# Hybrid decoder trunk on one core: queries and one more convolution projection by seven block products, query and key norms rearranged

## The chip, the core and the metric

The kernel runs on one core of a Trainium2 chip. A core has a matrix engine (TensorE, in the profile PE, with its weight loads as PEld), three engines for element-wise work (VectorE or DVE, ScalarE or ACT, GpSimd or POOL), a queue engine (SyncE or SP) and 16 DMA engines. Each engine works through its own list of instructions and waits for others by semaphores. The metric is the device time of one execution in microseconds; the shown time is the median of three runs.

## What is computed

Two layers. In each, a normalised input (512 tokens, 2048 channels) goes through one wide projection; three groups of heads (a short gated convolution, stick-breaking attention, gated linear attention) work on its parts, each result is gated, and an output projection adds it to the residual.

```python
h = rmsnorm(x, norm_g);  proj = h @ w_in                     # 2048 -> 7696 columns
y_conv = b * (conv3(c * h_) + bias) * silu(cv_g)             # 512 channels, width 3, causal
q = rmsnorm(sb_q, sb_qn_g); k = rmsnorm(sb_k, sb_kn_g)       # 8 heads of 128
z = (q * 128**-0.5) @ k.T                                    # in blocks of 128 queries, strictly causal
log_keep = where(mask, log_sigmoid(-z), 0)
later = reverse_cumsum(log_keep) - log_keep
w = where(mask, exp(log_sigmoid(z) + later), 0)
y_sb = (w @ v) * silu(sb_g)
y_gla = rmsnorm(gla(gl_q, gl_k, gl_v, decay)) * silu(gl_g)   # chunks of 64, with a state
out = x + concat(y_conv, y_sb, y_gla) @ w_out
```

All inputs and outputs are float32.

## The kernel before

**Projections.** Every operand of a projection is split into two float16 parts (high and low), and a product is three matmuls: high x high, high x low, low x high. A projection takes 256 output columns of a weight matrix ("v 0", "g 0", "conv h 1" and so on). Plain, it is 192 matmuls of 256 columns with tokens as rows (`project_toks`, through `tok_mm`, L683 to L685), or 96 of 512 columns with channels as rows (`project_cols`, L673 to L675). The projections named in `QUICK` and `QUICK_IN` go by seven block products in place of eight (`project_quick`, with `prod` at L764 for channels and L767 for tokens): 168 matmuls of 256 columns, or 336 of 128. Seven products need sums of the quarters of the weights (`wsums`), sums of the quarters of the input, made once per layer (`xsums`), and sums of the results (L778 to L792: three copies on ACT and five sums on DVE). In the input projection these are g, k of all four attention blocks, and "conv h 1".

**Weights.** A tile of weights (2 MB) is fetched from POOL's queue two projections ahead, into one of two buffers (`fetch`, L355). ACT sums its squares (L366), POOL reduces over partitions (L380), DVE makes the scale (L383 to L398). Then it is split: plain as two halves of 128x2048 (ACT L435, DVE L442); for seven products as seven parts of 128x1024 (ACT L485, DVE L486) with one accumulating DMA inside SBUF (L503) and three sums on DVE (L506, L508, L511). The parts lie in three pairs of buffers plus one (`w7h`, `w7l`), which the next projection's parts take as the matmuls free them.

**An attention block** (`for j in range(4)`) projects v, g, q and k of two heads. The squares of q and k are summed per head and token on ACT (L1318). `rsqrt_bits` makes the inverse roots on DVE from the bits of the number and three Newton steps (L211 to L218), once for q and once for k, eight columns each. q is multiplied by its roots (L1327), k by its roots and by `kg`, the product of the two norm weights (L1332, eight instructions). Both are split into float16 parts in one buffer, `qp`, (L1336, L1337) and transposed by DMA on SP (L1341). `attend` queues four steps that later projections start by `go()`: scores of each head and values of each head. Scores: query tiles are taken in two groups (`CHUNKS`): tiles 3 and 2 together (896 columns) and tiles 0 and 1 (384). Matmuls (L1226), a mask (L1230), two sigmoids per group with one scale per layer (L1234, L1236), a running product from the right (L1239), products and a split (L1241 to L1245), eight DMA transposes per block on SP (L1247). Values: matmuls (L1263) and a multiplication with the gate per group (L1270).

**The later convolution** (`conv_in(1)`, `conv_out(1)`) follows the last block: "conv h 1", "conv c 1", "conv g 1", "conv b 1". After the first of these `mixload` fetches the mixed results of the branches back from DRAM by six copies on SP (L887) into the buffers that hold `xsums`' sums until then. Before the output projection `weight_ratio` scales them (L1150, L1151).

**Order.** Apart from a part at the start that is written out by hand, a planner puts each engine's instructions into order at compile time, by its own estimate of times and by priorities (weights come first); on the chip the order is fixed.

Of the kernel before, what the change touches and what calls it, by code (L numbers as in the profile page):

```python
# [30 lines left out]
QUICK_IN = ("g 0", "k 0", "g 1", "k 1", "g 2", "k 2", "g 3", "k 3", "conv h 1")  # L31
# [5 lines left out]
TWICE = ("wm", "wgm", "wq", "ws", "wp", "vu", "bm", "bsmix", "gsmix", "lr", "xr0", "xrm", "xrt", "xtot", "xrstd", "xrs")  # L37


CHUNKS = ((((3, 0), (2, 512)), (3, 2)), (((0, 0), (1, 128)), (0, 1)))  # L40
# [3 lines left out]
def hybrid_trunk(ctx, tc, x, norm_g, w_in, conv_w, conv_b, sb_qn_g, sb_kn_g,  # L44
# [163 lines left out]
    def rsqrt_bits(dst, src, scale, n, tag):  # L208

        m = sm(n, tag + "rm")  # L210
        V.tensor_scalar(m, src, scale, EPS, ALU.mult, ALU.add)  # L211
        r = sm(n, tag + "r0")
        V.tensor_scalar(r.bitcast(I32), m.bitcast(I32), -0.5, float(0x5F375A86), ALU.mult, ALU.add)
        t = sm(n, tag + "rt")
        for i in range(3):
            V.tensor_tensor(t, r, r, ALU.mult)
            V.scalar_tensor_tensor(t, t, -0.5, m, ALU.mult, ALU.mult)
            V.scalar_tensor_tensor(dst if i == 2 else r, t, 1.5, r, ALU.add, ALU.mult)  # L218
# [68 lines left out]
    def layer_consts():  # L287
# [3 lines left out]
        for l in range(depth):  # L291
# [11 lines left out]
            V.tensor_scalar(gq[:, 0:1], gq[:, 0:1], gq[:, 1:2], 2.0 ** -10, ALU.mult, ALU.mult)  # L303
# [353 lines left out]
    for l in range(depth):  # L657
# [497 lines left out]
        def conv_in(j, then=lambda: None):  # L1155
# [5 lines left out]
            if j:  # L1161
                mixload()
# [3 lines left out]
            for c in range(2):  # L1166
                V.scalar_tensor_tensor(uc[:, c, :], ps[c], u, hb[:, c, :], ALU.mult, ALU.mult)
            y = wk([P, 2, seq], "kT")
# [45 lines left out]
        def attend(j, qT, kT, vh, vl, vu, g, s_):  # L1214
# [3 lines left out]
            def scores(hh):  # L1218

                th[hh] = wk([P, 2, 10, P], "th", 2, F16)  # L1220
                for n, (qtiles, _) in enumerate(CHUNKS):
# [12 lines left out]
                    S.activation(a, z[:, :zw], AF.Sigmoid, scale=nzun[:, l:l + 1])  # L1234
                    w = wk([P, zw], "zw")
                    S.activation(w, z[:, :zw], AF.Sigmoid, scale=zun[:, l:l + 1])  # L1236
# [12 lines left out]
            def values(hh):  # L1249
# [17 lines left out]
                for n, (_, cols) in enumerate(CHUNKS):  # L1267
                    q0 = min(cols)
                    a = op[:, 2 * n:2 * n + 2, :]
                    V.scalar_tensor_tensor(y[:, q0:q0 + 2, :], a[:, ::-1, :] if cols[0] > cols[1] else a, vu[:, 1:2],  # L1270
                                           g[:, hh, q0 * P:(q0 + 2) * P].rearrange("p (t c) -> p t c", c=P),
                                           ALU.mult, ALU.mult)
# [4 lines left out]
        for j in range(4):  # L1277
# [20 lines left out]
            for gain in (None, kg[:, l, :]):  # L1298
                raw = []

                def dst():
                    raw.append(wk([P, NT, GW], *(("raw", 1) if gain is None else ("kT",))))
# [7 lines left out]
                sq = sm(8, "qs")  # L1310
                for b in range(2):
# [4 lines left out]
                    for i in range(4):  # L1316
                        cs = slice(i * P, (i + 1) * P)
                        S.activation(e[:, cs], rb.rearrange("p a c -> p (a c)")[:, cs], AF.Square,  # L1318
                                     accum_out=sq[:, 4 * b + i:4 * b + i + 1])
                u2 = sm(1, "qu2")  # L1320
                V.tensor_scalar(u2, u, u, 1.0 / P, ALU.mult, ALU.mult)
                rs = sm(8, "qr")
                rsqrt_bits(rs, sq, u2, 8, "q")
                V.tensor_scalar(rs, rs, u, None, ALU.mult)
                if gain is None:
                    r8 = raw.rearrange("p a (h c) -> p (a h) c", c=P)
                    V.tensor_tensor(r8, r8, rs.rearrange("p (a o) -> p a o", o=1).to_broadcast([P, 8, P]), ALU.mult)  # L1327
                else:
                    for t in range(NT):
                        for hh in range(2):  # L1330
                            rp = raw[:, t, hh * P:(hh + 1) * P]
                            V.scalar_tensor_tensor(rp, rp, rs[:, 2 * t + hh:2 * t + hh + 1], gain, ALU.mult, ALU.mult)  # L1332

                top = 2.0 ** 10 if gain is None else 1.0
# [4 lines left out]
                nT_ = wk([P, 2, NT, 2, P], "kT" if qkT else "qT", dt=F16)  # L1339
# [4 lines left out]
            attend(j, *qkT, vh, vl, vu, g, s_)  # L1344
# [86 lines left out]
```

## Time and profile before

| | us |
|---|---|
| median of three runs (lowest, highest) | 1716.04 (1715.94, 1717.55) |
| profiled execution | 1717.69 |
| its span, from the first to the last instruction | 1715.9 |
| PE busy in it | 1669.9 |
| DVE busy | 1331.3 |
| ACT busy | 1129.1 |
| POOL busy | 239.2 |

Mean granted TensorE clock in the span: 0.992.

How to read the rows below. A row of a group is: line, engine, operation, out<-in by the program's names, shapes and count | busy us in total, mean ns of one | idle time of the engine just before them and what ended most of it. A row of the chain or of a timeline is: start in us from the span's start, duration, engine, line. A row of stages gives the stretch, its length, the busy us of each engine with its number of instructions, the granted clock, the share of the DMA engines and GB/s. Matmuls overlap in PE's pipeline: one of 256 columns is listed with 273 ns, but the next one starts 109 ns after it, so pace is read from starts.

### The profile page before, as it was taken

To read this page: it belongs to the slowest core of one execution; us is meant where nothing else is said; L and a number is where in the kernel's file an instruction comes from. 1 tells how busy PE (TensorE), PEld (TensorE's weight loads), DVE (VectorE), ACT (ScalarE), POOL (GpSimd) and SP (SyncE) were. 2 spreads that over 40 slices of the span, in tenths; PEclk is the share of its full clock that TensorE was granted. 3 is DMA by queue.
4 is the path that set the end of the run, shared out by engine and by line. 5 is a ranking of instruction groups with operands and counts; after the bars stand their busy time and mean duration, and the time that the engine had idled before them with its cause. 6 is when DMAs were issued, how large, how long until landed. Compare 5 with 4: busy or idle time off the path is not lost.

```text
span 1715.9 us, 36876 instructions
## 1 busy us (share of the span) xinstructions
PE 1669.9 (97%) x15642; PEld 1298.4 (76%) x15642; DVE 1331.3 (78%) x2327; ACT 1129.1 (66%) x1619; POOL 239.2 (14%) x286
## 2 busy tenths in 40 slices
PE   7999999999999989999989999999999999899999
PEld 5644548989898964799976455689898889548998
DVE  8975889877878767785688677997786888677883
ACT  7667677767666656666665676776765767565662
POOL 1211111111111111001122101121111111101110
PEclk9999999999999999999999999999999999999999
DMA  7233323566766686245543332446666667753441
GB/s 251 83 114 98 99 64 99 145 116 152 136 149 139 147 233 164 77 150 181 186 103 108 116 102 75 118 123 125 148 136 105 146 132 150 201 153 108 162 151 50
DMA packets 181478, 227.26 MB, mean 132 GB/s; under 512 B 94194, under 2 KB 141628, under 8 KB 180800
## 3 DMA queue, kind: packets, MB, share of 16 engines
q0 software_dynamic: 60352, 168.83, 34.4%
q1 hardware_dynamic: 111952, 46.61, 14.4%
q10 hardware_dynamic: 9008, 9.45, 1.7%
q8 instruction: 122, 2.00, 0.5%
q14 instruction: 44, 0.36, 0.1%
HBM read 179.65 MB, written 14.68 MB: 113 GB/s over the span
## 4 chain that ended last, share of the span: by engine, by line
PE 73%; DVE 12%; DMA 7%; ACT 4%; issue 3%; POOL 0%; DVEq 0%; ACTq 0%
PE psp L767 13%; PE psp L674 8%; PE psp L675 8%; PE psp L673 8%; PE psp L685 7%; PE psp L684 7%; PE psp L683 7%; PE psp L814 6%; PE psp L764 3%; DMA st<-in_w_in_dram 2%; DVE wl L486 2%; DMA th<-za 2%; DMA kT<-qp 2%; ACT junk L366 1%; DVE wl L442 1%
## 5 line engine op out<-in xcount | busy, mean ns | idle before, releaser
L366 ACT ACTIVATE junk<-st 128x2048 uint8<-128x2048 f32 x150 | 285.1, 1901 | 44.1 <-DMA st<-in_w_in_dram 42.8
L442 DVE SCALAR_TENSOR_TENSOR wl<-st,ws,wh 128x2048 f16<-128x2048 f32 x102 | 239.2, 2347 | 80.7 <-ACT wh L435 80.7
L435 ACT ACTIVATE wh<-st,ws 128x2048 f16<-128x2048 f32 x100 | 199.3, 1998 | 105.4 <-PE psp L674 47.1
L684 PE MATMUL psp<-wl,m 128*128 128x256 f16 x960 | 261.7, 273 | 0.0
L683 PE MATMUL psp<-wh,m 128*128 128x256 f16 x960 | 261.7, 273 | 0.0
L685 PE MATMUL psp<-wh,m 128*128 128x256 f16 x960 | 261.7, 273 | 0.0
L485 ACT ACTIVATE wh<-st,ws 128x1024 f16<-128x1024 f32 x150 | 167.6, 1143 | 120.5 <-DVE st L506 57.7
L486 DVE SCALAR_TENSOR_TENSOR wl<-st,ws,wh 128x1024 f16<-128x1024 f32 x150 | 189.6, 1279 | 27.4 <-ACT wh L485 27.3
L355 POOL DMA_DIRECT2D st<-in_w_in_dram x114 | 102.2, 900 | 436.0 <-DVE wl L442 319.4
L683 PE MATMUL psp<-wh,x 128*128 128x256 f16 x512 | 139.6, 273 | 0.0
L684 PE MATMUL psp<-wl,x 128*128 128x256 f16 x512 | 139.6, 273 | 0.0
L685 PE MATMUL psp<-wh,x 128*128 128x256 f16 x512 | 139.6, 273 | 0.0
L675 PE MATMUL psp<-x,wl 128*128 128x512 f16 x352 | 134.4, 382 | 2.2 <-DVE zun L186 2.2
L674 PE MATMUL psp<-x,wh 128*128 128x512 f16 x352 | 134.4, 382 | 0.0
L673 PE MATMUL psp<-x,wh 128*128 128x512 f16 x352 | 134.0, 381 | 0.0
L673 PE MATMUL psp<-m,wh 128*128 128x512 f16 x352 | 133.9, 380 | 0.0
L674 PE MATMUL psp<-m,wh 128*128 128x512 f16 x352 | 133.9, 380 | 0.0
L675 PE MATMUL psp<-m,wl 128*128 128x512 f16 x352 | 133.9, 380 | 0.0
L675 PEld LDWEIGHTS <-wl 128*128 128x128 f16 x704 | 69.2, 98 | 85.0 <-DVE wl L442 2.7
L673 PEld LDWEIGHTS <-wh 128*128 128x128 f16 x704 | 69.2, 98 | 81.5 <-issue 3.1
L380 POOL PARTITION_ALL_REDUCE wgm<-wm x75 | 40.0, 533 | 648.2 <-ACT junk L366 633.6
L674 PEld LDWEIGHTS <-wh 128*128 128x128 f16 x704 | 69.2, 98 | 80.8 <-issue 2.3
(427 smaller groups left out, 4042.2 us busy)
## 6 DMA issues: line engine op xcount, KB each, us to landing
st<-in_w_in_dram POOLq DMA_DIRECT2D x114, 1024.0 KB, 8.4
st<-in_w_out_dram POOLq DMA_DIRECT2D x32, 1024.0 KB, 7.4
st<-st POOLq DMA_DIRECT2D x18, 512.0 KB, 8.3
st<-in_w_in_dram SPq DMA_DIRECT2D x6, 1024.0 KB, 12.0
mixd<-g POOLq DMA_DIRECT2D x24, 256.0 KB, 7.7
x<-in_x_dram SPq DMA_DIRECT2D x4, 1024.0 KB, 4.9
qT<-in_x_dram ACTq DMA_DIRECT2D x8, 512.0 KB, 3.8
qT<-xs ACTq DMA_DIRECT2D x8, 512.0 KB, 3.9
```

What stands on the lines that cost most here:

```text
L366: sq = S.activation(junk(HK * GW).rearrange("p (k n) -> p k n", k=HK), staged[i][h], AF.Square, accum_out=peak[i][:, h:h + 1])
L435: hi = S.activation(wh[:, :, :GW], staged[i][h], AF.Copy, scale=scales[i])
L442: V.scalar_tensor_tensor(wl[:, :, :GW], staged[i][h], scales[i], wh[:, :, :GW], ALU.mult, ALU.subtract)
L485: hi = S.activation(h_, b, AF.Copy, scale=sc)
L486: V.scalar_tensor_tensor(l_, b, sc, h_, ALU.mult, ALU.subtract)
L673: T.matmul(o, wh[:, kk, cs], xh[:, :, k, :], start=st_, stop=False)
L674: T.matmul(o, wh[:, kk, cs], xl[:, :, k, :], start=False, stop=False)
L675: mm = T.matmul(o, wl[:, kk, cs], xh[:, :, k, :], start=False, stop=en)
L683: T.matmul(o, ah[:, t, k, :], wh[:, kk, :n], start=st_, stop=False, skip_group_check=True)
L684: T.matmul(o, ah[:, t, k, :], wl[:, kk, :n], start=False, stop=False, skip_group_check=True)
L685: return T.matmul(o, al[:, t, k, :], wh[:, kk, :n], start=False, stop=en, skip_group_check=True)
L767: mm = T.matmul(o[:, t * P:(t + 1) * P], a[p_][:, t, kk, :], w[q_][:, kk, :], start=st_, stop=en, skip_group_check=True)
```

## The change

- `QUICK_IN` gets q of all four blocks and "conv c 1": five more projections a layer, ten in all, go by seven products.
- `mixload` in `conv_in(1)` moves from behind "conv h 1" to behind "conv c 1" and its products with h.
- `kg` is multiplied onto q (one instruction on 128x1024) in place of q's inverse roots; k is multiplied by its own roots alone (one instruction in place of eight). Powers of two in the scales change with it.
- The sums of squares of q and k go into one tile of 16 columns, and one `rsqrt_bits` serves both.
- q's inverse roots, times the scale of the scores, and the same with the other sign, form a tile `qz` (16 columns). A sigmoid now takes its scale from `qz`, one value per query; so there is one sigmoid per query tile and sign in place of one per group and sign: 16 in place of 8 for the two heads of a block.
- The second group of query tiles is taken in the order 1, 0, so that the results of both groups lie in one order and one multiplication with the gate serves all four tiles.

```diff
-QUICK_IN = ("g 0", "k 0", "g 1", "k 1", "g 2", "k 2", "g 3", "k 3", "conv h 1")
+QUICK_IN = ("conv h 1", "conv c 1") + tuple(f"{n} {j}" for n in "gqk" for j in range(4))
-CHUNKS = ((((3, 0), (2, 512)), (3, 2)), (((0, 0), (1, 128)), (0, 1)))
+CHUNKS = ((((3, 0), (2, 512)), (3, 2)), (((1, 0), (0, 256)), (1, 0)))
@@ layer_consts
-            V.tensor_scalar(gq[:, 0:1], gq[:, 0:1], gq[:, 1:2], 2.0 ** -10, ALU.mult, ALU.mult)
+            V.tensor_scalar(gq[:, 0:1], gq[:, 0:1], gq[:, 1:2], 2.0 ** -21, ALU.mult, ALU.mult)
@@ conv_in
-            if j:
-                mixload()
             then()
             uc = wk([P, 2, seq], "raw", 1) if j else wk([P, 2, seq], "zw")
             ps, u = project(True, lambda: uc)
             for c in range(2):
                 V.scalar_tensor_tensor(uc[:, c, :], ps[c], u, hb[:, c, :], ALU.mult, ALU.mult)
+            if j:
+                mixload()
@@ scores
-                    S.activation(a, z[:, :zw], AF.Sigmoid, scale=nzun[:, l:l + 1])
                     w = wk([P, zw], "zw")
-                    S.activation(w, z[:, :zw], AF.Sigmoid, scale=zun[:, l:l + 1])
+                    for m, dst in ((0, a), (8, w)):
+                        for t, o in qtiles:
+                            ts_ = slice(o, o + (t + 1) * P)
+                            S.activation(dst[:, ts_], z[:, ts_], AF.Sigmoid,
+                                         scale=qz[:, m + 2 * t + hh:m + 2 * t + hh + 1])
@@ values
-                for n, (_, cols) in enumerate(CHUNKS):
-                    q0 = min(cols)
-                    a = op[:, 2 * n:2 * n + 2, :]
-                    V.scalar_tensor_tensor(y[:, q0:q0 + 2, :], a[:, ::-1, :] if cols[0] > cols[1] else a, vu[:, 1:2],
-                                           g[:, hh, q0 * P:(q0 + 2) * P].rearrange("p (t c) -> p t c", c=P),
-                                           ALU.mult, ALU.mult)
+                V.scalar_tensor_tensor(y, op[:, ::-1, :], vu[:, 1:2], g[:, hh, :].rearrange("p (t c) -> p t c", c=P),
+                                       ALU.mult, ALU.mult)
@@ the attention block
-            for gain in (None, kg[:, l, :]):
+            sq, rm = sm(16, "qs"), sm(16, "qrm")
+            for n in range(2):
...
-                rs = sm(8, "qr")
-                rsqrt_bits(rs, sq, u2, 8, "q")
-                V.tensor_scalar(rs, rs, u, None, ALU.mult)
-                if gain is None:
-                    r8 = raw.rearrange("p a (h c) -> p (a h) c", c=P)
-                    V.tensor_tensor(r8, r8, rs.rearrange("p (a o) -> p a o", o=1).to_broadcast([P, 8, P]), ALU.mult)
+                V.tensor_scalar(rm[:, 8 * n:8 * n + 8], sq[:, 8 * n:8 * n + 8], u2, EPS, ALU.mult, ALU.add)
+                r8 = raw.rearrange("p a (h c) -> p (a h) c", c=P)
+                if not n:
+                    qu = sm(1, "qu")
+                    V.tensor_scalar(qu, u, nzun[:, l:l + 1], 2.0 ** 25, ALU.mult, ALU.mult)
+                    by = kg[:, l, :].rearrange("p (o c) -> p o c", o=1)
                 else:
-                    for t in range(NT):
-                        for hh in range(2):
-                            rp = raw[:, t, hh * P:(hh + 1) * P]
-                            V.scalar_tensor_tensor(rp, rp, rs[:, 2 * t + hh:2 * t + hh + 1], gain, ALU.mult, ALU.mult)
-
-                top = 2.0 ** 10 if gain is None else 1.0
+                    rs = rsqrt_bits(rm, "q")
+                    qz = sm(16, "qz")
+                    V.tensor_scalar(qz[:, :8], rs[:, :8], qu, None, ALU.mult)
+                    V.tensor_scalar(qz[:, 8:], qz[:, :8], -1.0, None, ALU.mult)
+                    V.tensor_scalar(rs[:, 8:], rs[:, 8:], u, None, ALU.mult)
+                    by = rs[:, 8:].rearrange("p (a o) -> p a o", o=1)
+                V.tensor_tensor(r8, r8, by.to_broadcast([P, 8, P]), ALU.mult)
+
+                top = 2.0 ** 10 if n else 2.0 ** -14
```

`rsqrt_bits` keeps its three Newton steps; it now takes the mean squares from its caller and works on all columns of the tile that it is given.

21 lines of the change are left out of this document (10 added, 11 removed).

## The prediction

> **What bounds the kernel now.** I read the busy shares first, then the chain of work that ended last, then the same busy times cut into stages.
>
> ```profile
> PE 1669.9 (97%) x15642; PEld 1298.4 (76%) x15642; DVE 1331.3 (78%) x2327; ACT 1129.1 (66%) x1619; POOL 239.2 (14%) x286
> ...
> PE 73%; DVE 12%; DMA 7%; ACT 4%; issue 3%; POOL 0%; DVEq 0%; ACTq 0%
> PE psp L767 13%; PE psp L674 8%; PE psp L675 8%; PE psp L673 8%; PE psp L685 7%; PE psp L684 7%; PE psp L683 7%; PE psp L814 6%; PE psp L764 3%; DMA st<-in_w_in_dram 2%; DVE wl L486 2%; DMA th<-za 2%; DMA kT<-qp 2%; ACT junk L366 1%; DVE wl L442 1%
> ```
>
> TensorE is busy in 97% of the span and holds 73% of the chain, all of it in projections. A busy PE need not be a fast one, so I checked the pace at which matmuls start. The first row below is a piece of the chain (one key projection by seven products); the second one line's matmuls in one plain value projection, every third of its 192, with the first and last start; the third a plain gate projection in columns; the fourth 48 of the 168 matmuls of a gate projection by seven products.
>
> ```profile
> 327.73 18.76 PE psp L767 x336
> L683 PE MATMUL psp<-wh,x x64: 272/273/273, 519.1 to 539.7; 128*128 128x256 f16 x64
> 657.38:678.10 20.72, 20.72 (x99) 1.00 0.55 114
> 1300.37 5.24 PE psp L764 x48
> ```
>
> 336 matmuls of 128 columns in 18.76 us are 55.8 ns each. The plain one: 20.6 us over 63 steps of three matmuls, 109 ns for 256 columns; 64 steps are 20.9 us. Half the columns thus take 51% of the time, so short matmuls lose little. The PE runs at one pace, projection after projection, and what shortens its list shortens the span, as long as the others keep up. Whether they do is read from the stages (columns: wall time; busy us of PE, PEld, DVE, ACT, POOL with counts; granted clock; DMA share; GB/s):
>
> ```profile
> 260.00:346.00 86.00, 86.00 (x974) 77.78 (x973) 76.09 (x138) 63.85 (x109) 16.08 (x17) 1.00 0.45 118
> 433.00:519.00 86.00, 85.73 (x951) 77.87 (x949) 69.20 (x125) 59.71 (x94) 14.29 (x17) 1.00 0.67 145
> 1277.00:1370.00 93.00, 87.40 (x946) 79.08 (x944) 70.54 (x127) 60.29 (x97) 14.72 (x17) 0.98 0.72 134
> 600.00:620.00 20.00, 19.36 (x226) 17.53 (x224) 19.83 (x39) 17.85 (x32) 3.06 (x4) 1.00 0.60 154
> 620.00:640.00 20.00, 14.28 (x89) 8.54 (x88) 9.16 (x16) 8.45 (x9) 2.16 (x3) 0.96 1.10 288
> 640.00:660.00 20.00, 19.85 (x90) 9.07 (x90) 12.94 (x19) 10.00 (x11) 2.29 (x3) 0.87 0.75 209
> 1470.00:1490.00 20.00, 17.06 (x115) 11.03 (x113) 11.84 (x20) 10.41 (x10) 3.62 (x5) 1.00 1.09 307
> 1490.00:1510.00 20.00, 17.78 (x85) 8.46 (x85) 11.34 (x15) 9.41 (x10) 1.79 (x2) 0.91 0.73 219
> 1635.00:1654.00 19.00, 19.00 (x342) 18.89 (x340) 16.93 (x23) 12.63 (x15) 2.18 (x3) 1.00 0.52 168
> ```
>
> The second row is one attention block (v, g, q, k of one head pair) of the first layer: PE full, DVE 69.2 of 86. Two places lose PE time: a block of the second layer (5.6 us), and, in both layers, the place where the last attention block meets the later convolution (620 to 660, 1470 to 1510).
>
> **The change, part by part.**
>
> *PE.* Eight query projections (four a layer) go from 192 matmuls of 256 columns to 336 of 128: 20.9 - 18.76 = 2.2 us each, 17.3 us. Two projections "conv c 1" go from 20.72 to 168/48 x 5.24 = 18.34 us: 2.4 each, 4.8. Together 22.1 us. Nothing else moves on PE; the swapped order of the two small query tiles changes no column count.
>
> The Trainium skill ("TensorE: Matmul & The Clock Gate", Back-to-back issue gap) says that a real stream of weight loads and matmuls holds about 81 ns for 128 columns, against which a query by seven products would last 27.2 us and be a loss. This trace does not agree: 55.8 ns over 336 of them in the very kind of projection that is added.
>
> *DVE and ACT.* Rows of what is added and removed:
>
> ```profile
> L442 DVE SCALAR_TENSOR_TENSOR wl<-st,ws,wh 128x2048 f16<-128x2048 f32 x102 | 239.2, 2347 | 80.7 <-ACT wh L435 80.7
> L486 DVE SCALAR_TENSOR_TENSOR wl<-st,ws,wh 128x1024 f16<-128x1024 f32 x150 | 189.6, 1279 | 27.4 <-ACT wh L485 27.3
> L508 DVE TENSOR_TENSOR st<-st 128x1024 f32<-128x1024 f32 x18 | 22.0, 1222 | 0.5
> L788 DVE TENSOR_TENSOR g<-g 128x256 f32<-128x256 f32 x15 | 6.3, 423 | 0.4
> L218 DVE SCALAR_TENSOR_TENSOR qr<-qrt,qr 128x8 f32<-128x8 f32 x48 | 7.9, 165 | 1.4
> L1324 DVE TENSOR_SCALAR qr<-qr,wu 128x8 f32<-128x8 f32 x16 | 4.9, 308 | 0.3
> L1332 DVE SCALAR_TENSOR_TENSOR kT<-kT,qr,kg 128x128 f32<-128x128 f32 x64 | 17.5, 346 | 0.1
> L1327 DVE TENSOR_TENSOR raw<-raw,qr 128x1024 f32<-128x1024 f32 x8 | 9.8, 1225 | 0.3
> L1270 DVE SCALAR_TENSOR_TENSOR e<-psm,vu,g 128x256 f32<-128x256 f32 x32 | 13.9, 477 | 10.2 <-ACT e L1318 8.4 <-PE psm L1263 1.8
> ...
> L435 ACT ACTIVATE wh<-st,ws 128x2048 f16<-128x2048 f32 x100 | 199.3, 1998 | 105.4 <-PE psp L674 47.1 <-DVE ws L396 36.1 <-PE psp L767 10.7
> L485 ACT ACTIVATE wh<-st,ws 128x1024 f16<-128x1024 f32 x150 | 167.6, 1143 | 120.5 <-DVE st L506 57.7 <-DVE ws L396 25.5 <-PE psp L767 16.1
> L778 ACT ACTIVATE g<-psp 128x256 f32<-128x256 f32 x15 | 5.7, 382 | 0.0
> L1314 ACT ACTIVATE raw<-psp 128x512 f32<-128x512 f32 x16 | 9.2, 576 | 0.0
> L1234 ACT ACTIVATE za<-psz,nzun 128x896 f32<-128x896 f32 x16 | 15.9, 996 | 16.8 <-DMA th<-za 11.3 <-DVE psz L1230 5.5
> L1234 ACT ACTIVATE za<-psz,nzun 128x384 f32<-128x384 f32 x16 | 9.3, 578 | 0.7 <-DMA th<-za 0.7
> ```
>
> A projection that changes to seven products costs DVE seven splits, three sums of weight blocks and five small sums of results, and saves two long splits: 7 x 1.28 + 3 x 1.22 + 5 x 0.42 - 2 x 2.35 = +10.0 us. For ACT it is 7 x 1.14 + 3 x 0.38 - 2 x 2.00 = +5.1, less the two copies of a query out of PSUM (2 x 0.58): +4.0 for a query. DVE is paid back: one of two root chains per block (nine steps of 0.165, 1.5 us); eight multiplications of 0.346 against one like L1327's (2.77 - 1.23 = 1.5). The root multiples on 8 columns (0.3 each) come out about even; L1270's pair becomes one of twice the length, at most 0.95, so it saves 0 to 0.5 a head. Block net: DVE +7.0, to 76.2 us. ACT's sigmoids (two per head and pair of query tiles) become two per query tile: from the two L1234 rows a column costs 0.82 ns and a start 0.265 us, so four tiles (1280 columns) take 2.1 us instead of 1.57, twice per head, two heads: +2.1. ACT's block: 59.7 + 4.0 + 2.1 = 65.8.
>
> Against a block of 86.0 - 2.2 = 83.8 us DVE is at 91%, ACT at 79%. All of it is hidden behind PE only if DVE keeps no more than 7.6 of the 16.8 us that it idles per block today. Two rows bound what PE pays. At 1635 DVE does 16.93 of 19 us (89%) in a run of seven-product projections and PE loses nothing; at 260 it is 88% and PE is full: bound 0. At 600 DVE is at 99% (19.83 of 20) and PE loses 0.64 of 20, 3%: over eight blocks of 84 us, 21 us. The new 91% is nearest to the first: I take 1 us a block, 8.
>
> *Queries no longer wait for their inverse root* before their transposes, and sigmoids wait for both roots. The roots come right behind the keys' squares, and the keys' transposes stand between them and the scores: nothing on the path.
>
> *DMAs.* Each added projection issues one accumulating copy inside SBUF from POOL's queue; ten more.
>
> ```profile
> st<-st POOLq DMA_DIRECT2D x18, 512.0 KB, 8.3
> ```
>
> Its 8.3 us lie in the weight lead (a weight tile is fetched two projections, some 37 us, ahead), behind two splits that don't need it. I take 0; if the lead is gone it costs up to 8.3 us once, inside the bound above.
>
> *The reload of the mix moves* behind the second convolution projection, since the query sums occupy its room until then. It issues six copies on SP. Where it is now (SP's issues, then the chain at that place):
>
> ```profile
> 443.92 4.77 SPq L1341 DMA_TRANSPOSE kT<-qp  x2
> ...
> 617.17 7.09 SPq L887 DMA_DIRECT2D m<-mixd  x4
> 625.02 13.34 SPq L1341 DMA_TRANSPOSE kT<-qp  x2
> ...
> 654.81 22.61 SPq L1247 DMA_TRANSPOSE th<-za  x8
> ```
>
> ```profile
> 640.84 0.43 PE psp L673
> ...
> 645.49 0.22 PE psp L673
> ...
> 678.26 1.65 PE psm L1263 x18
> ```
>
> Four copies go ahead of the last block's key transposes, whose issue then takes 13.3 us instead of 4.8; the scores wait, PE is idle 5.7 us, and for some 5 us after that its matmuls take 0.43 us instead of 0.22. Moved, the copies no longer stand there. Bounds of the gain: 5.7 + (1 - 0.87) x 20 = 8.3 us in the first layer, 2.9 + 2.2 + 0.09 x 20 = 6.9 in the second, 15 together; or 0, if the transposes are late by DVE's own backlog (19.83 of 20 us just before). The extra 8.5 us of queueing are gone, but backlog grows by the second projection's +10 us: I take 9. What is queued behind the moved copies: the eight th transposes. They can be held by the copies' 7.1 us; the values that read them start on PE at 678, well after the first left at 655. Cost 0, at most 7 a layer.
>
> That a PE at rest restarts at half pace is also what the Trainium skill says ("TensorE: Matmul & The Clock Gate", Part 1: The HAM clock gate: an idle window of about 3.4 us drops the clock to half). The rows agree (clock 0.87; 0.43 against 0.22), and without it the gain's upper bound would be 11 us, not 15.
>
> **Sum.** -22.1 - 9 + 8 = -23.1 us. The profiled span is 1715.9, its execution 1717.7, the median of the runs 1716.0. I predict 1693.
>
> **Rivals.**
>
> *A. Slower: DVE's waits do not shrink.* It idles for other engines (DVE's idle 16.8 us per block). If they all stay, a block lasts 76.2 + 16.8 = 93 us: +7 x 8 = +56, less the 4.8 of the convolution: 1767. The point is 9.8 us of idle time kept per block; at 12 us it is 1729. For: each engine takes its own list in order, with scores, copies and splits in one list. Against: 89% at 1635 and 88% at 260 with a full PE. Chance 0.13; price taken 1740.
>
> *B. The stall at the convolution stays* (key transposes held by DVE's backlog), the rest as forecast: -22.1 + 8 = 1702. For: the 99% at 600. Chance 0.20.
>
> *C. DMA becomes the late one in the second layer.* There the share is 0.72 against 0.67 and a block already loses 5.6 us; ten accumulations more. Four blocks with 4 us more each: 1709. Chance 0.12.
>
> *D. All goes well:* no new stalls, the whole 15 us back: 1716 - 22 - 15 = 1679. Chance 0.12.
>
> *E. Weight loads bound the short matmuls.* A load takes 98 ns; unhidden, a query would last 33 us, +12 x 8: 1790.
>
> ```profile
> L767 PEld LDWEIGHTS <-s x192: 97/98/98, 330.2 to 343.5; 128*128 128x128 f16 x192
> ```
>
> The 18.76 us above speak against it: chance 0.01. By the 81 ns of the Trainium skill's page cited above it would be (27.2 - 20.9) x 8 = +50.
>
> **Numbers.** Forecast 0.42, A 0.13, B 0.20, C 0.12, D 0.12, E 0.01. The range 1679 to 1713 holds the forecast, B, nearly all of C and most of D, some 0.82. No change is within 0.2% (3.4 us), about what can be told. Faster: forecast, B, D and two thirds of C, 0.82; same 0.05 (the rest of C, the mild end of A); slower 0.13.
>
> **What would show it.** Queries as 336 matmuls in 18.8 us each, "conv c 1" in 18.4: the first term. Period from one key projection to the next near 84.5 us: the second. No gap before the last block's scores, clock 1.00 there, and the copies of the mix after the second convolution projection: the third. Wrong if PE waits on DVE splits or on sigmoids inside blocks (A), on DMA in the second layer (C), or if the values wait for th behind the copies.

## The result: 0.8% slower, and the profile after

The changed kernel takes 1729.27 us (median of 4 runs, 1726.94 to 1732.22) against 1715.99 (4 runs, 1714.73 to 1717.55): a ratio of 1.0078, 95% interval 1.0060 to 1.0096. The forecast was 1693 us. The profiled execution has a span of 1728.3 us.

The first row below is the page's busy shares of the changed kernel. The other rows are stages (columns as in the prediction): four attention blocks of the first layer, of the kernel before as their sum, of the changed one block by block with the sum.

```profile
PE 1661.5 (96%) x16938; PEld 1323.8 (77%) x16938; DVE 1397.8 (81%) x2321; ACT 1177.1 (68%) x1747; POOL 257.8 (15%) x296
```

```profile
sum 347.54, PE 345.54 PEld 313.54 DVE 285.12 ACT 243.12 POOL 59.00; mean PE 86.39 PEld 78.38 DVE 71.28 ACT 60.78 POOL 14.75
```

```profile
260.08:354.74 94.66, 89.15 (x1141) 82.72 (x1140) 84.90 (x144) 67.92 (x123) 17.85 (x19) 0.96 0.52 124
354.74:444.39 89.65, 84.34 (x1096) 77.94 (x1094) 73.99 (x117) 64.20 (x108) 15.32 (x16) 1.00 0.70 138
444.39:532.73 88.34, 85.62 (x1095) 79.50 (x1093) 75.42 (x121) 64.88 (x109) 16.02 (x17) 0.98 0.72 145
532.73:620.40 87.67, 84.17 (x1095) 77.94 (x1093) 77.31 (x124) 65.46 (x104) 16.01 (x16) 1.00 0.74 147
sum 360.32, PE 343.29 PEld 318.10 DVE 311.61 ACT 262.46 POOL 65.20; mean PE 85.82 PEld 79.52 DVE 77.90 ACT 65.62 POOL 16.30
```

By their shorter products the four blocks should have become 8.8 us shorter; they became 12.8 us longer (360.3 against 347.5). No helper engine is full: DVE idles 12.2 us a block, (360.32 - 311.61) / 4. Before, PE was busy for all but 2.0 of these 347.5 us; now it stands for 17.0, and some of the time in which it counts as busy it runs at half pace. What PE waited for in the whole span of the changed kernel (us in total, times, longest):

```profile
PE psp L767 <- ACT raw L778: 19.5, 8, 2.6
PE psp L767 <- DVE wl L486: 6.7, 4, 2.4
```

The first row is new: once per block, the third of a query's seven products waits for ACT's copy of the first out of PSUM (`raw` at L778). The two lie in the two halves of one PSUM bank (`pa` and `pd`). Before, its largest entry was the keys' transposes at the convolution:

```profile
PE psz L1226 <- DMA kT<-qp: 11.0, 2, 5.9
```

The chain of waits of the changed kernel shows one such query, in the second layer (start, duration, work):

```profile
1245.83 9.46 DMA th<-za
...
1256.45 1.16 ACT zw L1238 x2
1257.61 0.62 ACT za L1238 x2
1258.24 0.62 ACT zw L1238 x2
1258.86 1.22 ACT ga L836 x2
1260.08 1.12 ACT junk L366
1261.20 0.53 issue
1261.72 0.24 ACT junk L366
1261.97 0.28 ACT raw L778
1262.25 0.04 issue
1262.29 20.55 PE psp L767 x336
```

The transposes of one head's weights land; only then may the other head's sigmoids overwrite `za` (ACT idled 0.26 us for that, so the wait itself is small); behind them in ACT's list come the gate's sigmoids (L836), a square of the keys' weights (L366), and at last the copy, which takes 0.43 us, 0.28 of them in the chain, and lets PE go on. ACT works from 1255.4 us up to the copy almost without a pause: the copy is late because of what stands ahead of it in the list. From there 336 matmuls (the query's last five products and the keys' first two) take 20.55 us; at the full pace of the prediction's rows it would be 18.76. The cause of nearly all of that is the clock, in the section on the hardware.

At the convolution the changed kernel lost less, as forecast: two of its stages, then the stretch from the last key projection to the output projection, before and after. The convolution starts 15 and 18 us later here than before, so only the stretch compares the same work.

```profile
640.00:660.00 20.00, 18.50 (x163) 15.59 (x161) 17.40 (x26) 18.36 (x25) 2.20 (x3) 1.00 0.57 149
1490.00:1510.00 20.00, 17.13 (x155) 14.79 (x153) 16.10 (x24) 16.66 (x24) 2.19 (x3) 1.00 0.58 126
```

```profile
605.50:702.10 96.60, 90.08 (x520) 50.27 (x518) 66.15 (x118) 62.06 (x77) 11.83 (x16) 0.96 0.61 159
```

```profile
620.40:709.20 88.80, 85.16 (x592) 56.77 (x589) 66.01 (x118) 56.50 (x82) 11.59 (x15) 1.00 0.71 183
```

The stretch is 7.8 us shorter; 2.4 of them are the shorter products of "conv c 1", 5.4 the relief. Counted the same way the second layer gains 3.0 (95.1 to 89.65, less 2.4): 8.4 in all.

### The profile page after: what moved, and what is told of

It is laid out like the page before. It is cut to its first block, busy times and chain, and to the rows that moved or that the text cites. A ratio compares the mean times of both kernels' runs of the same rounds, so it can differ in the third digit from the quotient of the medians.

```text
span 1728.3 us, 39586 instructions
## 1 busy us (share of the span) xinstructions
PE 1661.5 (96%) x16938; PEld 1323.8 (77%) x16938; DVE 1397.8 (81%) x2321; ACT 1177.1 (68%) x1747; POOL 257.8 (15%) x296
## 4 chain that ended last, share of the span: by engine, by line
PE 37%; DVE 9%; DMA 4%; ACT 3%; issue 2%; POOL 0%; ACTq 0%; SPq 0%; DVEq 0%; POOLq 0%
PE psp L767 13%; PE psp L814 4%; PE psp L673 3%; PE psp L674 3%; PE psp L675 3%; PE psp L685 3%; PE psp L683 3%; PE psp L684 3%; DVE wl L486 2%; DMA th<-za 2%; PE psp L764 1%; ACT junk L366 1%; ACT wh L485 1%; DVE za L1242 1%; DMA st<-st 1%
## 5 line engine op out<-in xcount | busy, mean ns | idle before, releaser
L485 ACT ACTIVATE wh<-st,ws 128x1024 f16<-128x1024 f32 x210 | 234.2, 1144 | 134.6 <-DVE st L506 42.1
L366 ACT ACTIVATE junk<-st 128x2048 uint8<-128x2048 f32 x150 | 285.2, 1901 | 11.8 <-DMA m<-mixd 7.9
L486 DVE SCALAR_TENSOR_TENSOR wl<-st,ws,wh 128x1024 f16<-128x1024 f32 x210 | 266.9, 1280 | 30.5 <-ACT wh L485 30.1
L767 PE MATMUL psp<-wh,s 128*128 128x128 f16 x2048 | 190.1, 225 | 24.8 <-ACT raw L778 19.5
L767 PEld LDWEIGHTS <-s 128*128 128x128 f16 x3072 | 184.7, 101 | 32.1 <-issue 25.8
L684 PE MATMUL psp<-wl,m 128*128 128x256 f16 x704 | 193.1, 274 | 2.1 <-DVE wl L442 2.1
L683 PE MATMUL psp<-wh,m 128*128 128x256 f16 x704 | 193.0, 274 | 1.3 <-ACT wh L435 1.3
L685 PE MATMUL psp<-wh,m 128*128 128x256 f16 x704 | 193.2, 274 | 0.0
L767 PE MATMUL psp<-wl,s 128*128 128x128 f16 x1024 | 184.2, 225 | 5.0 <-DVE wl L486 4.7
L764 PE MATMUL psp<-s,wh 128*128 128x256 f16 x768 | 131.6, 273 | 2.4 <-ACT qT L778 1.7
L767 PEld LDWEIGHTS <-m 128*128 128x128 f16 x2160 | 122.6, 98 | 0.5 <-issue 0.3
L673 PE MATMUL psp<-m,wh 128*128 128x512 f16 x320 | 121.3, 379 | 0.8 <-DVE g L839 0.8
```

The lines of the kernel that those rows point to most:

```text
L366: sq = S.activation(junk(HK * GW).rearrange("p (k n) -> p k n", k=HK), staged[i][h], AF.Square, accum_out=peak[i][:, h:h + 1])
L485: hi = S.activation(h_, b, AF.Copy, scale=sc)
L486: V.scalar_tensor_tensor(l_, b, sc, h_, ALU.mult, ALU.subtract)
L673: T.matmul(o, wh[:, kk, cs], xh[:, :, k, :], start=st_, stop=False)
L683: T.matmul(o, ah[:, t, k, :], wh[:, kk, :n], start=st_, stop=False, skip_group_check=True)
L684: T.matmul(o, ah[:, t, k, :], wl[:, kk, :n], start=False, stop=False, skip_group_check=True)
```

## The experiments

Every run was timed beside the kernel before on the same chip; since that moved between 1716.4 and 1718.0 us from one set to the next, versions are compared by their ratios to it. Each edit also gives the planner another problem, so the lists of the engines differ in more places than the edit names. A profile is of one execution, which can lie off the median of its kernel: 15 us above it in n_move, 9 below in noq_two, 8 below in c_banks.

### Which part loses

**q_only**: the kernel before, with the queries by seven products and nothing else.

```diff
-QUICK_IN = ("g 0", "k 0", "g 1", "k 1", "g 2", "k 2", "g 3", "k 3", "conv h 1")
+QUICK_IN = ("conv h 1",) + tuple(f"{n} {j}" for n in "gqk" for j in range(4))
```

> The kernel before, with the four query projections a layer by seven products and nothing else changed. Theory 1 (a query's third product waits for ACT's copy of the first, which stands behind sigmoids and squares in ACT's list): the cost sits in the queries alone, so of the changed kernel's 35 us in the attention blocks at least 25 come back against 17.3 us of PE work saved: 1722 to 1736. Theory 2 (DVE's load decides): also slower, more so than the changed kernel, as its DVE list is 3 us a block longer: above 1736. Theory 3 (the split sigmoids and the merged roots cost the time): faster, about 1705.

1728.79 us (1726.52 to 1731.89), ratio 1.0065 (1.0046 to 1.0084): in the range of theory 1. The same wait stands at the top:

```profile
PE psp L767 <- ACT raw L778: 16.6, 8, 2.3
```

Here a head has two sigmoids per group of query tiles, as before the change, so the split sigmoids are not what makes the copy late. With 17.3 us less work on PE (by the prediction's count) and 11 more on the clock, the queries alone bring some 28 us of losses, by subtraction.

**c_only**: the later convolution's second group by seven products, `mixload` moved as in the change; queries and norms as before.

> The kernel before, with 'conv c 1' by seven products and the reload of the mix behind it, nothing else. If the relief at the convolution is the reload's: 1716 - 4.8 - 8.4 = 1703. If the second projection's splits eat it: 1711 or more.

1710.02 us (1704.23 to 1717.88), ratio 0.9957 (0.9935 to 0.9980). Its ratio is the lowest of all versions run, and it is the only part of the change that pays, though with some half of the gain expected. The mechanism of the relief is there all the same (PE waits 1.2 us for the keys' transposes, 11.0 before); its rows stand under the next run, which takes the move alone.

**mixload_only**: the kernel before, with only the call moved.

```diff
             for c in range(2):
                 S.activation(hb[:, c, :], ps[c], AF.Copy, scale=u)
-            if j:
-                mixload()
             then()
...
                 V.scalar_tensor_tensor(uc[:, c, :], ps[c], u, hb[:, c, :], ALU.mult, ALU.mult)
+            if j:
+                mixload()
```

> The kernel before with nothing but the reload moved behind the second convolution projection. By the stage rows of the changed kernel (8.4 us less there than before, beyond the shorter products): 1706 to 1711 us. Rival (the relief needs the other parts): 1713 to 1720 us.

1716.12 us (1712.53 to 1719.54), ratio 0.9993 (0.9976 to 1.0011): nothing. SP's queue says why, first in mixload_only, then in c_only:

```profile
618.75 7.26 SPq L887 DMA_DIRECT2D m<-mixd  x4
627.33 13.13 SPq L1341 DMA_TRANSPOSE kT<-qp  x2
640.64 1.01 SPq L887 DMA_DIRECT2D m<-mixd  x2
```

```profile
638.77 2.61 SPq L1341 DMA_TRANSPOSE kT<-qp  x2
...
657.61 1.00 SPq L887 DMA_DIRECT2D m<-mixd  x2
```

Moving the call did not move the copies: four of them still go ahead of the last keys' transposes. By the kernel's buffers they can leave as soon as their room, the input's sums, is free, and it is free after "conv h 1" as long as that is the last projection by seven products. Only "conv c 1" by seven products holds the room longer and so holds the copies back. The relief belongs to that part, not to the move.

**n_only**: the norm part alone (weights on queries, one root chain, split sigmoids, one gate multiplication), products and reload as before.

> The rearranged norms, sigmoids per query tile, merged roots and swapped tiles alone, with the projections by seven products and the reload as before. Theories 1 and 2: no change to 3 us better (DVE list 3 us a block shorter, PE never waited for it): 1713 to 1717. Theory 3: slower by 10 us or more.

1742.90 us (1733.73 to 1746.01), ratio 1.0141 (1.0117 to 1.0165): a miss by 26 us for theories 1 and 2, and what theory 3 gave.

```profile
PE psz L1226 <- DMA kT<-qp: 25.7, 4, 14.2
```

The keys' transposes are late. I took the reload for the cause and moved it.

**n_move**: n_only with the call of `mixload` moved.

> The norm rearrangement (weights on queries, one chain of inverse roots, split sigmoids) with the reload of the residual mix moved as in the change, and with the products of before (queries and the later convolution's second group by eight). Theory: the 26.9 us that the norm part lost by itself came from the reload standing between the two transposes at the convolution; with the reload behind them the norm part is worth within 6 us of nothing and the reload's relief (8 us) is kept: 1702 to 1714 us. Rival (the norm part stalls TensorE in the attention blocks whatever the reload does): 1730 us or more.

1736.70 us (1731.11 to 1751.91), ratio 1.0126 (1.0091 to 1.0161). The theory is not borne out, the time is in the rival's range, and after mixload_only it is plain why this run could not test the theory: the move alone moves no copy. The wait is still there.

```profile
PE psz L1226 <- DMA kT<-qp: 31.6, 6, 12.9
```

**no_q**: the changed kernel with the queries back to eight products.

```diff
-QUICK_IN = ("conv h 1", "conv c 1") + tuple(f"{n} {j}" for n in "gqk" for j in range(4))
+QUICK_IN = ("conv h 1", "conv c 1") + tuple(f"{n} {j}" for n in "gk" for j in range(4))
```

> The changed kernel with the queries back to eight products. Theory (the queries' third product waiting for the first one's copy is the main loss of the change): removing it gives back the queries' work, 17.6 us, and takes away some 30 us of stalls: 1700 to 1715 us. Rival (the loss lies in the norm part, and the queries only add to it): 1722 us or more.

1738.14 us (1729.25 to 1741.44), ratio 1.0102 (1.0076 to 1.0128): the theory misses, and the time is in the rival's range. Without the queries, and with the copies held back, the norm part costs 1.45% over c_only, some 25 us.

**qc**: queries and convolution group, reload moved, norms as before.

> Queries and the later convolution's second group by seven products, the reload moved, norms, scales and sigmoids as before (two PSUM banks a projection, as in the change). Theory 1 (the queries are the loss, the norm part adds nothing to them): about the changed kernel, 1723 to 1733 us, with TensorE waiting 15 us or more for the copy of a query's first product. Theory 2 (the norm part costs some 20 us in any company, as it did alone, with the reload moved and with the second group): 1700 to 1715 us. The same products with three banks gave 1738.75 us; below that by 6 us or more, the third bank is a loss here.

1720.89 us (1719.41 to 1724.91), ratio 1.0020 (0.9999 to 1.0041), 2 us below what theory 1 gave and not in the range of theory 2. The wait on the copy is there (16.2 us, 8 times). The change without its norm part is 0.58%, some 10 us, better than with it.

### What in the norm part

**noq_both**, **noq_roots**, **noq_two** start from no_q. noq_roots takes the inverse roots in two chains again, queries' own ahead of their multiplication with the weights:

```diff
                 if not n:
+                    rsq = rsqrt_bits(rm[:, :8], "qa")
                     qu = sm(1, "qu")
...
-                    rs = rsqrt_bits(rm, "q")
+                    rs = rsqrt_bits(rm[:, 8:], "q")
```

noq_two makes the gate multiplication in two instructions of two query tiles again; noq_both does both.

> The changed kernel with the queries back to eight products (1738 us), and with two pieces of the norm part undone: the inverse roots of queries and of keys in two chains again, and the gate multiplication in two instructions again (the split sigmoids and the weights on queries stay). If these two late links cost the norm part its 20 us (values waiting 8.1 us for the gate multiplication, scores 5.4 for the keys' transposes): 1715 to 1724 us. Rival (the eight sigmoids per head pair, for which scores wait 7.4 us, or the mere new order of the lists): 1730 us or more.

> The changed kernel with queries by eight products (1738 us) and the inverse roots in two chains again; the gate multiplication stays merged. Both pieces undone gave 1712.9. If the late roots (keys' transposes late, scores waiting) are the piece: 1710 to 1718 us. If the merged gate multiplication is: 1730 us or more.

> The changed kernel with queries by eight products (1738 us) and the gate multiplication in two instructions again; the roots stay in one chain. If the merged gate multiplication is the piece (values waiting 8.1 us for it): 1710 to 1718 us. If the roots are: 1730 us or more. In between in both: they share it.

noq_both 1712.91 us (1707.56 to 1721.45), ratio 0.9975 (0.9953 to 0.9997); noq_roots 1714.33 (1704.46 to 1724.80), 0.9983 (0.9959 to 1.0008); noq_two 1731.57 (1722.09 to 1739.61), 1.0088 (1.0059 to 1.0117). With the queries by eight products it is the one root chain, then: undoing it alone gives back 1.2%, some 20 us, and undoing the merged gate multiplication alone gives nothing that could be told. PE's first waits in no_q, then the first in noq_roots:

```profile
PE psm L1266 <- DVE e L1270: 8.1, 3, 3.8
PE psz L1226 <- ACT zw L1238: 7.4, 3, 4.1
```

```profile
PE psm L1266 <- DVE e L1270: 9.5, 3, 3.8
```

The wait for the merged gate multiplication stays and costs little. The scores' wait for sigmoids (7.4 us, down to 0.5 in noq_roots) goes with the joint chain, as it would if the scale of every sigmoid, which comes only with the keys' squares, were late. But the profile of noq_two, which keeps the joint chain, does not show that wait, and has one of 8.3 us for weights at the first output projection in its place. (That profile is of the shortest of its eight runs.) So what the joint chain makes late is not settled; that undoing it gives back the 20 us is.

**a_both**: the whole change with both pieces undone.

> The changed kernel with the inverse roots of queries and keys in two chains again and the gate multiplication in two instructions again. If the two pieces cost as much beside quick queries as they did without them (25 us): 1700 to 1710 us. If they cost only what the norm part adds to queries and convolution group (8 us): 1716 to 1724 us. If nothing: 1726 us or more.

1733.60 us (1730.38 to 1737.00), ratio 1.0102 (1.0074 to 1.0130): not better than the change (1.0078). Beside quick queries nothing could be won back by undoing the two pieces: PE stands at the queries first (19.6 us for the copy), and one new wait of 7.8 us for weights at an output projection has come in. So undoing them does not give back the 10 us by which the change is above qc; which piece, or which new order of the lists, costs these was not found.

### Can the queries' wait be taken away

**banks**: the changed kernel with three PSUM banks per projection of seven products, so that the third and fourth product need not wait for the copy of the first.

```diff
-            (pa, pd), (pb, pf) = ([bk[:, n * GW:(n + 1) * GW] for n in range(2)]
-                                  for bk in [bank(psp, "p") for _ in range(2)])
+            ba, bb, bd = (bank(psp, "p") for _ in range(3))
+            pa, pb, pd, pf = ba[:, :GW], bb[:, :GW], bd[:, :GW], bd[:, GW:]
...
-            prod(pd, wT3, a11_21, False)
-            S.activation(y22, zd, AF.Copy)
+            prod(pd, wT3, a11_21, True)
             prod(pf, w22, a12_s, False)
-            prod(pa, w21, a12, False)
+            S.activation(y22, zd, AF.Copy)
+            prod(pa, w21, a12, False, True)
```

> The changed kernel with the four sums of a seven-product projection in three PSUM banks instead of two (first sum and second sum a bank each, third and fourth share one), and ACT's copy of the third emitted after the fourth product: the third and fourth product then wait for no copy. Theory 1: the waits for ACT's copy (19.5 us in eight queries) and the half pace after them (some 6 us) go: 1703 to 1710. Theory 2: PE waits at the next place instead, 1723 to 1730.

1718.75 us (1715.90 to 1728.24), ratio 1.0009 (0.9992 to 1.0027): 0.7% below the change, some 12 us: between the two ranges, 9 us short of theory 1.

**qc_banks** and **c_banks**: the same three banks in qc and in c_only.

> Queries and the later convolution's second group by seven products, the reload moved, norms as before, and three PSUM banks for each projection of seven products, so that its third product need not wait for the copy of its first. If the wait on that copy is the main loss and the norm part is neutral: 1705 to 1716 us. Rival (the queries' loss sits in DVE's extra sums and differences, which the banks leave): 1720 us or more.

> The later convolution's second group by seven products, the reload moved, three PSUM banks for each projection of seven products, queries by eight and norms as before. With the same edit without the third bank at 1710 us: if keys, gates and convolution groups wait little for their first product's copy, 1704 to 1711 us; a third bank that takes slots from the projections of eight would show as 1715 us or more.

qc_banks 1738.75 us (1737.00 to 1741.08), ratio 1.0122 (1.0102 to 1.0141), 1.0% above qc; c_banks 1735.93 (1728.18 to 1745.12), 1.0109 (1.0079 to 1.0138), 1.5% above c_only. Both miss the first range and fall in the rival's, and in both a new wait has come in; PE's first rows in banks, in qc_banks and in c_banks:

```profile
PE psp L767 <- ACT wh L485: 11.2, 6, 3.5
```

```profile
PE psp L767 <- DVE raw L789: 15.5, 8, 2.1
PE psp L767 <- DVE wl L486: 12.1, 8, 2.5
```

```profile
PE psp L767 <- ACT raw L1314: 12.1, 6, 3.0
```

The wait for a query's copy is down to 0.8 us in banks and qc_banks (c_banks has plain queries), but a product now waits for another copy or sum out of PSUM (L789 on DVE; L1314 is ACT's copy of the plain query), or for its weight parts (L485, L486). The kernel has three such banks in all (`psp`), so a projection that takes all three leaves none free for the next one, which fits the waits at L789 and L1314. Why the trade pays in one kernel and not in the others is not settled.

**q_dve**: the changed kernel, with DVE making the copy of a query's first product.

```diff
-            S.activation(y12, za, AF.Copy)
+            if isq[0]:
+                V.tensor_copy(y12, za)
+            else:
+                S.activation(y12, za, AF.Copy)
```

> The changed kernel, with the copy of a query's first product made by VectorE in place of ScalarE. If TensorE waits because the copy stands behind weight squares and sigmoids in ScalarE's list, the wait on it (19.5 us, 8 times) shrinks to under 6 us and the time falls to 1703 to 1718 us. Rival (VectorE, 81% busy, takes the copy as late): a wait of the same size on VectorE and 1724 us or more.

1739.35 us (1737.74 to 1741.19), ratio 1.0129 (1.0093 to 1.0165). The wait on the copy does shrink, to 2.5 us, but the time rises, which neither side expected together: PE now waits for low weight parts.

```profile
PE psp L769 <- DVE wl L486: 27.4, 10, 3.5
```

**a_hook** puts both squares of the next weights (the keys') behind the copy in ACT's list; **a_half** and **qc_half** only the second one. Nothing else is asked of the planner.

```diff
+            y12_ = S.activation(y12, za, AF.Copy)
+            if isq[0]:
+                hook(y12_)
```

```diff
             order(wmax(i, 0), mm)
+            if isq[0]:
+                rest.append(i)
...
+            y12_ = S.activation(y12, za, AF.Copy)
+            if rest:
+                with tc.high_priority():
+                    order(wmax(rest.pop(), 1), y12_)
```

> The changed kernel with the two squares of the keys' weights placed behind the copy of a query's first product in ScalarE's list. If the copy is late because of the squares, TensorE's wait on it falls from 19.5 us to under 10, and the time to 1712 to 1722 us. Rival (the squares are then late themselves, and with them the keys' weight parts): waits on weight parts grow by as much, 1726 us or more.

> The changed kernel with the second square of the keys' weights placed behind the copy of a query's first product in ScalarE's list; the first square stays ahead. In the profile of the change that square took 1.9 of the 2.7 us for which TensorE stood, and the copy takes 0.4. If the copy's place is the loss: the wait on it falls from 19.5 us to some 8, and with the half-clock windows that such a stall opens the time falls to 1711 to 1720 us. Rival (the keys' weight chain bounds the stage, so that any delay to it is paid in full): 1729 us or more.

> Queries and the later convolution's second group by seven products, the reload moved, norms as before (1720.9 us), with the second square of the keys' weights behind the copy of a query's first product. If the copy's place is the loss: the wait on it falls from 16.2 us to under 8, and the time to 1703 to 1714 us, faster than before. Rival (weight chain): 1720 us or more.

a_hook 1767.99 us (1756.65 to 1772.34), ratio 1.0288 (1.0249 to 1.0327); a_half 1741.32 (1734.09 to 1743.91), 1.0131 (1.0107 to 1.0154); qc_half 1728.71 (1726.26 to 1735.68), 1.0074 (1.0050 to 1.0097). Each does to the wait what was expected (4.6 us of it are left in a_hook) and loses all the same. Waits for the copy and for low weight parts, PE in a_half, then in qc_half:

```profile
PE psp L770 <- DVE wl L489: 20.0, 10, 2.4
PE psp L770 <- ACT raw L781: 7.6, 8, 2.0
```

```profile
PE psp L770 <- DVE wl L489: 23.2, 9, 3.5
...
PE psp L770 <- ACT raw L781: 4.6, 5, 1.8
```

In a_half, what 12 us are taken from the copy comes back as 13 at the weight parts, and more in other places. In a_hook PE's largest new wait is for a sum that DVE makes, and DVE stands for the accumulating copy of the weights (PE's row, then DVE's in the changed kernel and in a_hook):

```profile
PE psp L769 <- DVE raw L796: 22.4, 6, 5.3
```

```profile
DVE st L506 <- DMA st<-st: 6.1, 5, 2.0
```

```profile
DVE st L506 <- DMA st<-st: 29.7, 8, 5.4
```

The rival holds in time, and in a_half and qc_half by the waits that it named; in a_hook the late weights reach PE by way of DVE's list. Squares, scale, accumulating copy, splits and products of the keys' weights form one chain, and in these runs it has no lead. A square that waits for the copy delays it; the copy that waits for the square stops PE. One of the two pays.

## Why the prediction was wrong

**PE's work, -22.1 us: right.** The trace has just the matmuls that the term counted (x16938 against x15642; 2688 more of 128 columns, 1200 fewer of 256 and 192 fewer of 512), and short ones keep their pace: without its one window at half pace (1.6 us, last section) the stretch of 336 shown above takes 18.9 us, 18.76 forecast.

**DVE's and ACT's added work: right.** A block was to have 76.2 us on DVE and 65.8 on ACT; the block at 444 has 75.4 and 64.9, the next one 77.3 and 65.5.

**The relief at the convolution, -9 us: the size was right (8.4), the step that gave it was half right.** The copies do go behind the keys' transposes, but because "conv c 1" by seven products keeps their room, as mixload_only shows; the rest of the sentence, that the moved call no longer stands there, would not have held by itself.

**New stalls, 1 us per block: this is the step that failed.** From the spans, 1728.3 - 1715.9 = 12.4 = -22.1 - 8.4 + 42.9: the losses that are left over were 43, not 8. Of these, 34.5 lie in the eight blocks, 4.3 each: the four of the first layer became 12.8 us longer and the four of the second 4.4, where 17.3 less was due. Some 22 of them are time in which PE stands, some 10, by estimate, are half pace (seven windows of 3.41 us at clock 0.50 in the blocks, one before). The other 8.4 lie outside the blocks, where no term looked; 5.0 of them at the first projection of the output, right behind the relief, which lasts 25.9 us in place of 21.0: PE waits 2.1 us for weight parts in it, and the granted clock is 0.87. The price was read from DVE's share, with two rows at 88 and 89% where PE lost nothing. Neither row has scores in it: the one at 1635 is a run of projections by seven products and nothing else, the one at 260 the first block, with two of its four projections plain. The share was right and says nothing about order. In a block, the small copy that frees a PSUM bank stands in ACT's list behind whatever the planner put ahead of it, and once the first product is done PE has just the second, 48 x 55.8 ns = 2.7 us, and a few matmuls of the values in hand until it needs the bank. The Trainium skill ("PSUM — Partial Sum Buffer", PSUM bank collisions raise a hardware error) says that PSUM is to be guarded by bank and not by address. The trace agrees: the 19.5 us are waits of a product that writes the other half of the bank, and with a bank of its own (banks) it waits 0.8. That removing this wait won back 12 us at most, and in most versions nothing, points to several links without lead in the blocks, of which this wait is one.

**The accumulating copies, 0 us as long as the weight lead is there: the lead was gone.** DVE's wait for them is 6.1 us in the changed kernel (0.3 before) and 29.7 in a_hook, which is 2.1% slower than the change, some 36 us. How much of these waits PE paid was not measured.

**The norm rearrangement, "nothing on the path": wrong without quick queries, small with them.** The roots of both in one chain cost some 20 us there (noq_roots). In the whole change undoing them gives nothing back (a_both); that the queries' own stalls hide this loss is a guess, and the 10 us that the norm part costs there remain unexplained.

**The rivals.** A, at 0.13, came nearest. Its mechanism was named as "each engine takes its own list in order, with scores, copies and splits in one list", and that is what the runs show, but for ACT's list more than for DVE's. Its arithmetic puts 12 us of kept idle time per block at 1729 us, blocks 17.6 us longer in all; measured are 12.2, 17.2 and 1729.3. That the sum agrees to the microsecond is luck: A left out the relief of 8.4 us, and the losses outside the blocks are as large. It had its chance from the 88 and 89% rows, the same that priced the stalls. B, C, D and E did not occur: the clock at the convolution is 1.00, the second layer's blocks lose no more than the first's, and short matmuls keep their pace. The 1790 us of E also count the queries' saving twice: the forecast without that saving is 1710, and the same condition then gives some 1806.

## What to carry to other kernels

A share of some 90% on a helper engine is harmless where all its work has slack (89% at 1635 before), and costly where a small instruction that frees a buffer stands behind large ones in the same list (ACT at 73% of a block here): ask for each buffer that the bound engine reuses how much work the engine has in hand until then, and what may stand ahead of the release. When three projections that need split weights follow each other, price the chain that prepares the weights (here squares, scale, accumulating copy, splits), not each engine's sum; before, a plain query stood between two of them, and PE waited 1.3 us for the low parts of weights (L767 on L486) in place of 6.7. And parts that each look free can cancel or hide each other, so run them alone and in pairs: here the only part that won was one small one, at 0.9957.

## What the runs showed of the hardware

Stalls of equal length can cost different amounts of clock. Six of the eight stalls at queries took 2.58 to 2.60 us each; three halved the clock for the 3.41 us that followed, three did not. Four of them, each as a pair of 3.41 us windows of the changed kernel, with the stall in the first:

```profile
495.27:498.68 3.41, 1.38 (x25) 1.38 (x25) 3.38 (x6) 3.41 (x5) 1.53 (x2) 1.00 0.00 0
498.68:502.09 3.41, 3.41 (x36) 3.41 (x34) 3.41 (x8) 1.25 (x3) 1.25 (x2) 0.50 0.79 88
584.01:587.42 3.41, 1.93 (x35) 1.93 (x35) 3.38 (x5) 3.41 (x6) 2.08 (x2) 1.00 0.02 5
587.42:590.83 3.41, 3.41 (x65) 3.41 (x63) 3.41 (x8) 0.69 (x2) 1.26 (x3) 1.00 1.14 107
1259.86:1263.27 3.41, 0.98 (x18) 0.97 (x18) 3.38 (x6) 3.41 (x6) 0.88 (x2) 1.00 0.01 2
1263.27:1266.68 3.41, 3.41 (x36) 3.41 (x34) 3.41 (x7) 1.26 (x3) 1.59 (x2) 0.50 0.59 67
1348.60:1352.01 3.41, 1.53 (x28) 1.53 (x28) 3.38 (x6) 3.41 (x5) 1.69 (x2) 1.00 0.01 2
1352.01:1355.42 3.41, 3.41 (x65) 3.41 (x63) 3.41 (x8) 1.09 (x3) 1.36 (x2) 1.00 0.84 89
```

After windows in which PE worked for 0.98 or 1.38 us the clock is 0.50 and 36 matmuls fit in the next window; after 1.53 or 1.93 us it stays at 1.00 with 65. What decides is how much of the stall falls into one window of a fixed grid. The grid shows in the clock records: the half-paced windows begin at 498.68, 1263.27 and 1440.76 us (the third behind another of the six), 224 and 52 times 3.4133 us apart. The rule holds for all windows of this grid in the changed kernel that start at full clock, one at 14 us, in the first microseconds of the kernel, aside: behind all eleven in which PE was busy for 1.38 us or less the clock is 0.50, behind all others it stays at 1.00. The Trainium skill ("TensorE: Matmul & The Clock Gate", Part 1: The HAM clock gate) speaks of an idle window of about 3.4 us. The trace differs: here a window that was idle for 2.0 us did it. Such a stall then costs 1.6 us more than its length, (65 - 36) x 55.8 ns.
